# A hybrid attention and gated-DeltaNet layer: the 32-to-64 merge of the triangular inverses, four chunks at a time instead of one

## The chip, the cores and the metric

The kernel runs on one core of a Trainium2 chip. The metric is device time in microseconds (us) of one execution; the runs of the kernel before have a median of 1288.59 us (1287.44 to 1289.28, three runs). PE is the matrix engine, PEld its loading of the stationary operand, DVE, ACT and POOL are the vector, scalar and general engines, and SP is the engine whose queue issues most of the DMAs. "Lnnn" is a line of the kernel before.

## What is computed

One layer works on 1024 tokens of 1024 features. Two mixers share a normed input: a chunked band attention (8 heads of 64) and a gated DeltaNet (4 heads of 128). The change concerns the DeltaNet. Per chunk and head it needs

```
t_mat = a_strict + eye(CHUNK)                     # unit lower triangular
value       = triangular_solve(t_mat, v_beta)
k_cumdecay  = triangular_solve(t_mat, k_beta * exp(decay))
# then, chunk after chunk:
v_new = val - kc @ S
o     = qd @ S + att @ v_new
S     = S * cd + kt.T @ v_new
```

The reference uses chunks of 64 tokens, the kernel chunks of 128 (8 chunks, `c` = 0 to 7). In place of two triangular solves the kernel forms the inverse of the 128 x 128 matrix for each head, and multiplies by it. An output projection and a feed-forward part of width 4096 follow.

## The kernel before, in words

All matrix products of the big projections are done as three products of high and low parts. The program runs in four parts: the projections; attention beside the delta recurrence; the output projection; the feed-forward part. Everything below is in the first two.

**Two interleavings.** `interleave` takes turns among generators by the costs that they yield and a weight each. The first one runs the projections (`dq`, `dv`, gate, `ak`, `aq`, the first six tiles of `av`) with weight 1 and `delta_prep` with weight 0.35. The second one runs `attention` (weight 1), `delta_all` (2.0) and the last tiles of `av` (2.5). The order so written is a priority: a planner that simulates the program at build time then fixes the order of the instructions on every engine, and each engine's queue, SP's among them, works through that order strictly. An instruction later in the program can be put earlier where its operands and buffers are ready and the engine would stand idle.

**The inverse.** `delta_prep` computes the strict triangle A of each chunk, writes it to DRAM (`a_dr`, L521), reads the sixteen-per-chunk 32 x 32 diagonal blocks back (`ad`, L531), inverts all of them at once on DVE (L539, L543: 31 steps), and writes the inverses X and their transposes Y to DRAM (`x_dr`, `y_dr`, L548; 128-byte pieces). `delta_merge(c)` then makes the whole transposed inverse of one chunk:

- It loads A (L557, 256 KB), X and Y (L559, 64 KB each), clears the 128 x 512 page `m_yb` on POOL (L560) and copies the four diagonal blocks of Y into it (L563).
- From 32 to 64: the product p1 (L568, four matmuls, one per head, for the upper pair of blocks, then four for the lower pair), each half copied out by ACT (L570), and p2 (L577, the same numbers), each half written to `m_yb` by ACT with its sign turned (L578). A matmul is 32 x 32 or 64 x 32 of the array. It is executed as two records in the trace.
- From 64 to 128: transposes and products (L582, L584), a copy (L587), p4 (L592) and a last ACT write (L594).

Each chunk thus has four groups of eight records of the 32-wide form. A group and the ACT copy of its bank take turns, because both touch one PSUM bank. `m_p`, `m_tp`, `m_s`, `m_yb`, `m_ab` are the names of these tiles in the profile (p1, p2 and p4 are all `m_p`).

**The recurrence.** `delta_all` steps chunk by chunk through `delta_state` (S: `c_pk`, `c_pv`, `c_pq`, `c_pS`, all at L461 through the helper `four`), `delta_out` of the chunk before (O: `c_mt`, `c_po`), `delta_fin` (F: `c_tpo`), the merge of the next chunk (M) and the first step, that is the loads, of the merge after that (L), in the order of the string `ORDER = "OSMOSMFSOMOSMSL"`. All delta products share the two PSUM banks of `ps_d`. `c_pv` of chunk c reads the merged inverse of chunk c.

**Attention beside it.** `t_sb` and `t_sa` (L793) are scores, `t_tpb` and `t_tpa` (L844, L855) transposes, `t_o` (L865) values; `t_o` uses half of the array's columns (128*64 in the profile). Its queries are loaded as `t_q` (L774) on SP's queue.

Of the kernel before, what the change touches and what calls it, by code (L numbers as in the profile page):

```python
# [18 lines left out]
NT = SEQ // P  # L19
# [22 lines left out]
NV = 6  # L42
WV = 2.5
# [3 lines left out]
def hymba_kernel(  # L47
# [20 lines left out]
    nc = tc.nc  # L68
# [43 lines left out]
    ident = cpool.tile([P, P], F32, name="ident")  # L112
# [292 lines left out]
    def att_proj(u, col, kind, res=None):  # L405
        w = load_block(col, f"wa{kind}")
        for t in range(NT):
# [77 lines left out]
    def sumsq(sq, st, tp, n):  # L485
        nc.scalar.activation(sq, tp, AF.Square)
        ss = small(st, n + "_ss", 4)
        nc.vector.tensor_reduce(ss, b4(sq), AX.X, ALU.add)
        return ss
# [57 lines left out]
            for h in range(4):  # L547
                nc.sync.dma_start(out=dst[:, :, h, :], in_=src.rearrange("(q h) r e -> h q r e", h=4)[h])  # L548

    def delta_merge(c, res):  # L550

        n = f"m{c}"
        Ap, Yp, s1 = (page("pp", n + k) for k in ("_ab", "_yb", "_s1"))
        A, Y = b4(Ap), b4(Yp)
        X = s1[:, 384:512].rearrange("p (h e) -> p h e", h=4)
        Yc = s1[:, 256:384].rearrange("p (h e) -> p h e", h=4)
        nc.sync.dma_start(out=Ap, in_=a_dr[c])  # L557
        for dst, src in ((X, x_dr), (Yc, y_dr)):
            nc.sync.dma_start(out=dst, in_=src[4 * c:4 * c + 4].rearrange("b r h e -> (b r) h e"))  # L559
        nc.gpsimd.memset(Yp, 0.0)  # L560
        for b in range(4):
            bs = slice(32 * b, 32 * b + 32)
            nc.gpsimd.tensor_copy(Y[bs, :, bs], Yc[bs])  # L563
        yield 0
        p1 = bank(ps_d, n + "_p1")
        for c0 in (0, 64):
            for h in range(4):
                nc.tensor.matmul(p1[c0:c0 + 32, 32 * h:32 * h + 32], A[c0:c0 + 64, h, c0:c0 + 32],  # L568
                                 Y[c0:c0 + 64, h, c0 + 32:c0 + 64], start=True, stop=True)
            nc.scalar.copy(s1[c0:c0 + 32, 0:128], p1[c0:c0 + 32, 0:128])  # L570
        yield 500
        p2 = bank(ps_d, n + "_p2")
        for c0 in (0, 64):
            cs = slice(c0, c0 + 32)
            for h in range(4):
                hs = slice(32 * h, 32 * h + 32)
                nc.tensor.matmul(p2[cs, hs], X[cs, h, :], s1[cs, hs], start=True, stop=True)  # L577
            nc.scalar.mul(Y[cs, :, c0 + 32:c0 + 64], p2[cs, 0:128].rearrange("p (h e) -> p h e", h=4), -1.0)  # L578
        yield 500
        tp = bank(ps_d, n + "_tp")  # L580
        for h in range(4):
            nc.tensor.transpose(tp[0:64, h * 64:h * 64 + 64], Y[0:64, h, 0:64], ident[0:64, 0:64])  # L582
        for h in range(4):
            nc.tensor.matmul(tp[0:64, 256 + h * 64:320 + h * 64], A[64:128, h, 0:64], Y[64:128, h, 64:128],  # L584
                             start=True, stop=True)
        x1 = s1
        nc.scalar.copy(x1[0:64, :], tp[0:64, :])  # L587
        yield 700
        p4 = bank(ps_d, n + "_p4")
        for h in range(4):  # L590
            hs = slice(h * 64, h * 64 + 64)
            nc.tensor.matmul(p4[0:64, hs], x1[0:64, hs], x1[0:64, 256 + h * 64:320 + h * 64],  # L592
                             start=True, stop=True)
        nc.scalar.mul(Y[0:64, :, 64:128], p4[0:64, 0:256].rearrange("p (h e) -> p h e", h=4), -1.0)  # L594
        res[c] = Yp
        yield 400
# [90 lines left out]
    def delta_all(ab, kTs):  # L687

        Ys, D = {}, {}
        merge = delta_merge(0, Ys)  # L690
        yield from merge
        merge = delta_merge(1, Ys)
# [653 lines left out]
    for _ in delta_proj(u, DK, 4, "dk", None, kT, w_dk, first):  # L1346
        pass
    ab = ab_proj(u)
    after = []
# [58 lines left out]
```

## Time and profile before

| | |
|---|---|
| median of the runs | 1288.59 us (1287.44 to 1289.28) |
| the profiled execution: its own time | 1288.31 us |
| its span in the trace | 1286.6 us |
| mean granted TensorE clock | 0.998 |
| PE busy | 1260.6 us, 6702 records |
| DVE, ACT, POOL busy | 935.0, 553.9, 293.0 us |
| the merges' 32-wide groups: first and last start | 264.4 and 504.7 us |
| attention beside the recurrence | about 364 to 575 us |

The profiler records one execution. Times in its views count from the start of the span. In a timeline row the first number is the start, the second the length from the first record's start to the last one's end, then engine, line, operation, out<-in, the array's rows*columns in use, the operand's shape and the count. Records on PE overlap, so that the pace of PE is read from start to start, not from the durations.

### The profile page before, as it was taken

How to read it: one execution, taken by the hardware profiler on the slowest of the kernel's cores; microseconds unless marked ns; L12 is line 12 of the kernel's file. 1: busy time of each engine (PE TensorE's matmuls, PEld its weight loads, DVE VectorE, ACT ScalarE, POOL GpSimd, SP SyncE). 2: the span in 40 equal slices, each digit the busy share in tenths (PEclk: the TensorE clock that was granted, in tenths of full speed). 3: DMA queues.
4: the chain of work that ended last, by engine and by line, in shares of the span. 5: the costliest groups of instructions: out<-in, count | busy, mean ns of one | idle time of the engine just before them, and what ended most of it. 6: DMA issues, size and time to landing. Idle time of an engine off the chain costs nothing.

```text
span 1286.6 us, 18043 instructions
## 1 busy us (share of the span) xinstructions
PE 1260.6 (98%) x6702; PEld 1040.6 (81%) x6702; DVE 935.0 (73%) x1401; ACT 553.9 (43%) x919; POOL 293.0 (23%) x499
## 2 busy tenths in 40 slices
PE   9999999999999999989999999999999999999998
PEld 7778878788888887868877788888887888888886
DVE  7899987665046666863529876776668997897988
ACT  7233132133166664665335445444455443333331
POOL 4435461454024355523310000000000000000034
PEclk9999999999999999999999999999999999999999
DMA  6214353656492742125351433232358733422002
GB/s 223 61 44 140 100 164 112 145 147 160 144 270 79 218 109 75 42 65 163 122 166 31 151 116 129 98 110 97 105 196 318 238 93 104 131 86 95 17 33 98
DMA packets 129288, 160.65 MB, mean 125 GB/s; under 512 B 22832, under 2 KB 71984, under 8 KB 128688
## 3 DMA queue, kind: packets, MB, share of 16 engines
q1 hardware_dynamic: 111104, 137.20, 34.7%
q10 hardware_dynamic: 18096, 22.29, 5.0%
q8 instruction: 53, 0.87, 0.3%
q14 instruction: 35, 0.29, 0.1%
HBM read 111.75 MB, written 47.71 MB: 124 GB/s over the span
## 4 chain that ended last, share of the span: by engine, by line
PE 72%; DVE 8%; issue 2%; DMA 2%; POOL 1%; ACT 1%; POOLq 1%; SPq 0%; ACTq 0%; DVEq 0%
PE q L1087 22%; PE p L1183 20%; PE op L166 5%; PE av_ps L166 3%; PE aq_ps L166 3%; PE g_ps L166 3%; PE t_o L865 3%; PE ak_ps L166 2%; PE t_sb L793 1%; PE t_sa L793 1%; PE t_tpb L844 1%; PE t_tpa L855 1%; PE c_mt L461 1%; PE c_pS L461 1%; DVE ml L148 1%
## 5 line engine op out<-in xcount | busy, mean ns | idle before, releaser
L1255 POOL TENSOR_TENSOR y<-y,y 128x1024 f32<-128x1024 f32 x6 | 19.3, 3243 | 591.7 <-DVE y L1251 572.9
L1251 DVE TENSOR_TENSOR y<-y,p 128x1024 f32<-128x1024 f32 x46 | 55.2, 1218 | 5.4 <-PE p L1183 4.5
L808 DVE CUSTOM_DVE_ANT_0 t_pb<-t_sb,biasn 128x256 f32<-128x256 f32 (+1 forms) x64 | 25.4, 402 | 43.6 <-POOL biasn L720 25.4
L166 PE MATMUL op<-mh,wo_h 128*128 128x512 f32 x128 | 50.3, 393 | 0.8 <-DVE t_nm L808 0.3
L166 PE MATMUL op<-ml,wo_h 128*128 128x512 f32 x128 | 50.1, 391 | 0.0
L166 PE MATMUL op<-mh,wo_l 128*128 128x512 f32 x128 | 48.3, 391 | 0.0
L823 ACT ACTIVATE t_pb<-t_pb,t_nm 128x256 f32<-128x256 f32 (+1 forms) x64 | 31.6, 494 | 22.7 <-DVE t_nm L817 12.7
L966 DVE TENSOR_TENSOR h<-op,op_x 128x512 f32<-128x512 f32 x16 | 10.8, 688 | 30.7 <-PE op L166 30.7
L793 PE MATMUL t_sb<-ks,t_q 128*128 128x256 f32 (+1 forms) x144 | 30.4, 308 | 0.8 <-DMA t_q<-q_dr 0.5
L973 POOL TENSOR_TENSOR op_q<-op_q 128x512 f32<-128x512 f32 x14 | 20.1, 1439 | 48.0 <-ACT op_q L972 47.8
L166 PEld LDWEIGHTS op<-mh,wo_h 128*128 128x128 f32 x128 | 24.0, 188 | 7.4 <-issue 1.0
L817 DVE CUSTOM_DVE_ANT_0 t_pa<-t_sa,biaso,t_nm 128x384 f32<-128x384 f32 (+2 forms) x48 | 26.3, 547 | 4.4 <-PE t_sa L793 2.9
L865 PE MATMUL t_o<-t_ta,vt 128*64 128x128 f32 x240 | 27.3, 293 | 1.4 <-DVE t_ta L858 1.1
L166 PEld LDWEIGHTS op<-mh,wo_l 128*128 128x128 f32 x128 | 24.0, 188 | 5.2 <-issue 0.2
L166 PEld LDWEIGHTS op<-ml,wo_h 128*128 128x128 f32 x128 | 24.0, 188 | 4.9
L166 PE MATMUL g_ps<-uh,wg_h 128*128 128x512 f32 x64 | 25.2, 394 | 1.4 <-ACT wg_h L147 1.4
L826 ACT ACTIVATE t_pa<-t_pa,t_nm 128x384 f32<-128x384 f32 (+2 forms) x48 | 26.4, 550 | 0.1
L793 PE MATMUL t_sa<-ks,t_q 128*128 128x256 f32 (+2 forms) x128 | 25.5, 310 | 0.3 <-DVE t_nm L808 0.3
L166 PE MATMUL g_ps<-uh,wg_l 128*128 128x512 f32 x64 | 25.2, 394 | 0.4 <-POOL wg_l L148 0.4
L166 PE MATMUL dq_ps<-uh,wdq_h 128*128 128x512 f32 x64 | 25.5, 398 | 0.0
L166 PE MATMUL dv_ps<-uh,wdv_l 128*128 128x512 f32 x64 | 25.4, 397 | 0.0
L166 PE MATMUL aq_ps<-waq_h,uh 128*128 128x512 f32 x64 | 25.3, 401 | 0.0
(1102 smaller groups left out, 4353.8 us busy)
## 6 DMA issues: line engine op xcount, KB each, us to landing
wa<-in_w_ff_dram SPq DMA_DIRECT2D x32, 512.0 KB
a<-in_w_ff_dram SPq DMA_DIRECT2D x32, 512.0 KB
b<-f_dr SPq DMA_DIRECT2D x32, 512.0 KB
f_dr<-yy ACTq DMA_DIRECT2D x16, 512.0 KB
t_q<-q_dr SPq DMA_DIRECT2D x30, 256.0 KB
f_dr<-zz ACTq DMA_DIRECT2D x13, 512.0 KB
ks<-k_dr SPq DMA_DIRECT2D x16, 256.0 KB
wo_r<-in_w_out_dram SPq DMA_DIRECT2D x16, 256.0 KB
```

The source lines that it names most:

```text
L166: nc.tensor.matmul(ps, a, b, start=(i == 0), stop=(i == n - 1))
L461: nc.tensor.matmul(ps[:, hs], lhs(h, hs), rhs(h, hs), start=True, stop=True)
L793: nc.tensor.matmul(o, q[m][:, i * P:(i + 1) * P], k[:, c], start=(m == 0), stop=(m == 1))
L808: nc.vector.tensor_tensor_reduce(sb[:, c], bk[:, c], new[g][pp][:, c], -1.0, 3.0e38, ALU.add, ALU.min, nm[:, 4 + i:5 + i])
L817: nc.vector.tensor_tensor_reduce(sa[e][:, 0:wa], bk[:, 0:wa], old[g][i][:, 384 - wa:384], -1.0, nm[:, 4 + i:5 + i], ALU.add, ALU.min, nm[: ...
L823: nc.scalar.activation(sb[:, c], sb[:, c], AF.Exp, bias=m, scale=-1.0, accum_out=T["sums"][:, 4 + i:5 + i])
L826: nc.scalar.activation(sa[e][:, 0:wa], sa[e][:, 0:wa], AF.Exp, bias=m, scale=-1.0, accum_out=T["sums"][:, i:i + 1])
L865: nc.tensor.matmul(po[64 * e:64 * e + 64, pp * P:(pp + 1) * P], vt[k0 + j][:, 64 * h:64 * h + 64], (ta[e] if j < na else tb)[:, c:c + P], ...
L973: nc.gpsimd.tensor_tensor(acc, acc, sq, ALU.add)
L1087: nc.tensor.matmul(part(ps, q), l[:, s], r, start=(k + m == 0), stop=(k == 3 and m == 2))
L1183: nc.tensor.matmul(part(ps[q], 0) if by_rows else part(ps[q // 2], q % 2), l[:, s], part(r, k), start=(i + k + m == 0), stop=(i + k + m == 4))
L1251: nc.vector.tensor_tensor(y[i][m], y[i][m], ps[m], op)
```

## The change

`delta_merge` is split. A new generator `delta_low(b, W, tag)` does the step from 32 to 64 for the four chunks 4b to 4b+3 together. It clears two pages W on POOL, and loads with 32 DMAs on SP's queue: sixteen 32-row blocks of Y straight into their places in W, eight of X, and eight 32 x 32-per-head blocks of A (128-byte pieces, except X with 512). Then p1 is 16 matmuls for r0 = 0 and, after ACT's copy, 16 for r0 = 64, and p2 the same. The helper `held` puts the other 15 of such a group behind the first on PE's queue, at high priority. ACT copies 32 x 512 at once, and writes -p2 into W.

`delta_merge(c)` keeps the step from 64 to 128. It takes its operands from W, loads the lower left quarter of A (one DMA, 64 rows), and fills the final page `m_yb` with one POOL clear of 64 x 256 and two POOL copies of 64 x 256.

`delta_low(0)` is chained behind `delta_prep` in the first interleaving, with its pages from `pp`; `delta_low(1)` is chained ahead of the merge of chunk 4 in `delta_all` at c = 2, with its two working pages from `wh`.

```
+    def held(args, step):
+        first = step(*args[0])
+        with tc.issue_after(first.ins), tc.high_priority():
+            for a in args[1:]:
+                step(*a)
+
+    def delta_low(b, W, tag):
+        W += [page("pp", f"{n}_w{i}") for i in range(2)]
+        xa, s1 = page(tag, n + "_xa"), page(tag, n + "_s1")
...
+        for i in range(2):
+            nc.gpsimd.memset(W[-2 + i], 0.0)
+        for c in range(4):
+            q = 16 * b + 4 * c
+            for k in range(4):
+                nc.sync.dma_start(out=Y[c // 2][32 * k:32 * k + 32, c % 2, :, 32 * (k % 2):32 * (k % 2) + 32],
+                                  in_=y_dr[q + k])
+            for r0 in (0, 64):
+                nc.sync.dma_start(out=XA[r0:r0 + 32, c], in_=x_dr[q + r0 // 32])
+                nc.sync.dma_start(out=XA[r0 + 32:r0 + 64, c], in_=a4[c, r0 + 32:r0 + 64, :, r0:r0 + 32])
+        yield 0
+        places = [(c, h, slice(128 * c + 32 * h, 128 * c + 32 * h + 32)) for c in (3, 2, 1, 0) for h in range(4)]
+        p1 = bank(ps_d, n + "_p1")
+        for r0 in (0, 64):
+            rs, rs2 = slice(r0, r0 + 32), slice(r0 + 32, r0 + 64)
+            held(places, lambda c, h, hs: nc.tensor.matmul(
+                p1[rs, hs], XA[rs2, c, h, :], Y[c // 2][rs2, c % 2, h, 32:64], start=True, stop=True))
+            nc.scalar.copy(s1[rs], p1[rs])
+        yield 1000
+        p2 = bank(ps_d, n + "_p2")
+        for r0 in (0, 64):
+            rs = slice(r0, r0 + 32)
+            held(places, lambda c, h, hs: nc.tensor.matmul(
+                p2[rs, hs], XA[rs, c, h, :], s1[rs, hs], start=True, stop=True))
+            for i in range(2):
+                nc.scalar.mul(Y[i][rs, :, :, 32:64],
+                              p2[rs, 256 * i:256 * i + 256].rearrange("p (c h e) -> p c h e", c=2, h=4), -1.0)
+        yield 1000

-    def delta_merge(c, res):
+    def delta_merge(c, W, res):
...
+        nc.sync.dma_start(out=A[64:128], in_=a_dr[c].rearrange("r (h e) -> r h e", h=4)[64:128, :, 0:64])
+        nc.gpsimd.memset(Y[64:128, :, 0:64], 0.0)
+        nc.gpsimd.tensor_copy(Y[0:64, :, 0:64], Yd[0:64])
+        nc.gpsimd.tensor_copy(Y[64:128, :, 64:128], Yd[64:128])
...
-            merge = delta_merge(c + 2, Ys) if c + 2 < NT else iter(())
+            merge = delta_merge(c + 2, W, Ys) if c + 2 < NT else iter(())
+            if c == 2:
+                merge = chained(delta_low(1, W, "wh"), merge)
...
-        (delta_prep(kT, ab), 0.35))
-    interleave((attention(after[NV - 1]), 1.0), (delta_all(ab, kT), 2.0), (values, WV))
+        (chained(delta_prep(kT, ab), delta_low(0, W, "pp")), 0.35))
+    interleave((attention(after[NV - 1]), 1.0), (delta_all(ab, kT, W), 2.0), (values, WV))
```

More of the change, by code (lines that the diff above doesn't have):

```diff
@@ L548, in delta_prep @@
                 nc.sync.dma_start(out=dst[:, :, h, :], in_=src.rearrange("(q h) r e -> h q r e", h=4)[h])
-    def delta_merge(c, res):
-        n = f"m{c}"
[L553 to L563, printed above, removed]
-        yield 0
[L565 to L579, printed above, removed]
@@ new lines, in held @@
+    def held(args, step):
[4 more added lines that the diff above has]
+    def delta_low(b, W, tag):
+        n = f"l{b}"
+        W += [page("pp", f"{n}_w{i}") for i in range(2)]
+        xa, s1 = page(tag, n + "_xa"), page(tag, n + "_s1")
+        XA = xa.rearrange("p (c h e) -> p c h e", c=4, h=4)
+        Y = [w.rearrange("p (c h e) -> p c h e", c=2, h=4) for w in W[-2:]]
+        a4 = a_dr[4 * b:4 * b + 4].rearrange("c r (h e) -> c r h e", h=4)
+        for i in range(2):
[26 more added lines that the diff above has]
+        yield 1000
@@ new lines, in delta_merge @@
+    def delta_merge(c, W, res):
+        n = f"m{c}"
+        Yp, sa = page("pp", n + "_yb"), page("pp", n + "_sa")
+        Y = b4(Yp)
+        A = sa[:, 0:256].rearrange("p (h e) -> p h e", h=4)
+        Yd = W[c // 2].rearrange("p (c h e) -> p c h e", c=2, h=4)[:, c % 2]
+        nc.sync.dma_start(out=A[64:128], in_=a_dr[c].rearrange("r (h e) -> r h e", h=4)[64:128, :, 0:64])
+        nc.gpsimd.memset(Y[64:128, :, 0:64], 0.0)
+        nc.gpsimd.tensor_copy(Y[0:64, :, 0:64], Yd[0:64])
+        nc.gpsimd.tensor_copy(Y[64:128, :, 64:128], Yd[64:128])
+        yield 0
@@ L580, in delta_merge @@
         tp = bank(ps_d, n + "_tp")
         for h in range(4):
-            nc.tensor.transpose(tp[0:64, h * 64:h * 64 + 64], Y[0:64, h, 0:64], ident[0:64, 0:64])
+            nc.tensor.transpose(tp[0:64, h * 64:h * 64 + 64], Yd[0:64, h, :], ident[0:64, 0:64])
         for h in range(4):
-            nc.tensor.matmul(tp[0:64, 256 + h * 64:320 + h * 64], A[64:128, h, 0:64], Y[64:128, h, 64:128],
+            nc.tensor.matmul(tp[0:64, 256 + h * 64:320 + h * 64], A[64:128, h, :], Yd[64:128, h, :],
@@ L585, in delta_merge @@
                              start=True, stop=True)
-        x1 = s1
-        nc.scalar.copy(x1[0:64, :], tp[0:64, :])
+        nc.scalar.copy(sa[0:64, :], tp[0:64, :])
         yield 700
@@ L591, in delta_merge @@
             hs = slice(h * 64, h * 64 + 64)
-            nc.tensor.matmul(p4[0:64, hs], x1[0:64, hs], x1[0:64, 256 + h * 64:320 + h * 64],
+            nc.tensor.matmul(p4[0:64, hs], sa[0:64, hs], sa[0:64, 256 + h * 64:320 + h * 64],
                              start=True, stop=True)
@@ L685, in delta_fin, with delta_all @@
         yield 500
-    def delta_all(ab, kTs):
+    def delta_all(ab, kTs, W):
         Ys, D = {}, {}
-        merge = delta_merge(0, Ys)
-        yield from merge
-        merge = delta_merge(1, Ys)
+        yield from delta_merge(0, W, Ys)
+        merge = delta_merge(1, W, Ys)
         for c in range(NT + LATE):
@@ L1348, in hymba_kernel @@
     ab = ab_proj(u)
+    W = []
     after = []
```

## The prediction, made before the change was run

> **What bounds the kernel now.** I read the page's busy shares first, then the busy time by stretches of the stages that the change touches.
>
> ```profile
> PE 1260.6 (98%) x6702; PEld 1040.6 (81%) x6702; DVE 935.0 (73%) x1401; ACT 553.9 (43%) x919; POOL 293.0 (23%) x499
> ```
>
> ```profile
> 245.00:364.00 119.00, 119.00 (x590) 96.46 (x589) 46.92 (x110) 33.87 (x65) 43.40 (x67) 1.00 0.63 172
> 364.00:440.00 76.00, 76.00 (x741) 64.95 (x740) 46.09 (x160) 48.37 (x146) 27.93 (x74) 1.00 0.59 173
> 440.00:520.00 80.00, 76.31 (x743) 65.47 (x742) 52.44 (x159) 46.52 (x143) 39.11 (x100) 1.00 0.35 97
> 520.00:575.00 55.00, 50.01 (x422) 41.51 (x421) 41.77 (x111) 35.97 (x97) 22.03 (x61) 0.97 0.17 50
> ```
>
> The second fence gives stretch, length, then busy PE, PEld, DVE, ACT, POOL, granted clock, DMA share, GB/s. From 245 to 440 us PE has no idle time. From 440 to 575 it idles 3.7 and 5.0 us. No other engine comes near its limit there. So the time of these stages is PE's, and the question is what the merges' small matmuls cost on PE. Third, the merges' own instructions (busy times per record: minimum, median, maximum, in ns; first and last start).
>
> ```profile
> L568 PE MATMUL m_p<-m_yb,m_ab x128: 192/193/213, 264.4 to 501.4; 64*32 64x32 f32 x128
> L577 PE MATMUL m_p<-m_s x128: 191/191/212, 283.4 to 504.7; 32*32 32x32 f32 x128
> L570 ACT COPY m_s<-m_p x16: 249/256/258, 270.5 to 501.6; 32x128 f32<-32x128 f32 x16
> L578 ACT ACTIVATE m_yb<-m_p x16: 249/268/269, 318.0 to 504.9; 32x128 f32<-32x128 f32 x16
> ```
>
> 256 records in groups of 8 make 32 groups, four a chunk, all inside the stretch where PE is the bound.
>
> **The price of one group.** It is read from start to start in PE's timeline.
>
> ```profile
> 410.25 1.06 PE L461 MATMUL c_pk<-state,kT 128*128 128x128 f32 x8
> 411.24 0.43 PE L577 MATMUL m_p<-m_s 32*32 32x32 f32 x8
> 411.60 0.51 PE L793 MATMUL t_sb<-ks,t_q 128*128 128x256 f32 x2
> ...
> 509.04 1.06 PE L461 MATMUL c_po<-c_vn,c_att 128*128 128x128 f32 x8
> 509.94 0.38 PE L855 MATMUL t_tpa<-ident,t_pa 128*128 128x128 f32 x2
> ```
>
> A group takes 411.60 - 411.24 = 0.36 us until the next work starts. The eight `c_pk` ahead of it took 411.24 - 410.25 = 0.99, while eight equal matmuls before work of their own form took 509.94 - 509.04 = 0.90: 0.09 more, which I read as the array running empty before it changes its form. Behind a group, the next one pays as well:
>
> ```profile
> 370.24 0.66 PE L865 MATMUL t_o<-t_tb,vt 128*64 128x128 f32 x8
> 370.83 0.43 PE L577 MATMUL m_p<-m_s 32*32 32x32 f32 x8
> 371.19 1.16 PE L461 MATMUL c_pq<-state,c_jq 128*128 128x128 f32 x8
> ...
> 366.23 0.43 PE L568 MATMUL m_p<-m_yb,m_ab 64*32 64x32 f32 x8
> ...
> 481.44 0.44 PE L568 MATMUL m_p<-m_yb,m_ab 64*32 64x32 f32 x8
> ```
>
> `c_pq` is 1.16 long behind a group where `c_po` was 1.06: 0.10. One visit to the 32-wide form thus costs 0.09 + 0.36 + 0.10 = 0.55 us. Inside it the records follow at (0.43 - 0.19) / 7 = 0.034 us, so eight of them are only 0.27 us. The rest, 0.28 us, is paid per visit whatever its length.
>
> **Part by part.**
>
> *PE.* Before: 32 visits x 0.55 = 17.6 us. Eight of them (366.23 the first, 481.44 the last) stand beside a `t_o` of the 128*64 form, where the array would have to change its form anyway; there I take off 0.2, 1.6 us in all: 16.0. After: the same 128 matmuls, 256 records, in 8 visits of 32: p1 and p2, two halves each, twice. The halves stay apart, because ACT's copy and the next half share a bank. A visit is 0.09 + (31 x 0.034 + 0.19 - 0.07) + 0.10 = 1.36 us (0.07 is 0.43 - 0.36, what the next work overlaps): 10.9 us. Gain 5.1. If the visits beside `t_o` saved nothing, it would be 6.7; if the planner lets other work into the held groups and 16 visits result, about 16.0 - 13.1 = 2.9.
>
> *Waits of PE in the merges of the last chunks.*
>
> ```profile
> PE m_p L577 <- ACT m_yb L578: 0.8, 2, 0.4
> PE m_p L577 <- DVE c5q_ss L488: 0.5, 1, 0.5
> PE m_p L568 <- ACT m_s L570: 0.3, 1, 0.3
> ```
>
> These 1.6 us (us, times, longest) arise where little work is left to fill PE and p1, copy, p1, copy, p2 of one chunk follow each other. After the change chunks 4 to 7 are done at about chunk 3's turn, where PE never idles. I take half, 0.8 us, as gained: other waits will appear in their place. Bounds 0 and 1.6.
>
> *ACT.* Removed 16 x 0.256 + 16 x 0.268 = 8.4 us. Added: 4 copies of 32x512 and 8 writes of 32x256; the nearest rows are a 64x512 copy and a 64x256 write.
>
> ```profile
> L587 ACT COPY m_s<-m_tp x8: 567/578/580, 356.4 to 509.0; 64x512 f32<-64x512 f32 x8
> L594 ACT ACTIVATE m_yb<-m_p x8: 363/377/378, 362.4 to 514.6; 64x256 f32<-64x256 f32 x8
> L560 POOL MEMSET m_yb<- x8: 520/526/532, 247.1 to 478.6; 128x512 f32 x8
> L563 POOL COPY m_yb<-m_s x32: 279/286/293, 254.7 to 481.0; 32x128 f32<-32x128 f32 x32
> ```
>
> 4 x 0.578 + 8 x 0.377 = 5.3 us. ACT idles 28 of 76 us from 364 to 440: nothing either way on the path.
>
> *POOL.* Removed 8 x 0.526 + 32 x 0.286 = 13.4 us. Added: 4 clears of 0.526, 8 smaller ones of at most that, and 16 copies of 256 columns, between 0.286 and twice that: at most 2.1 + 4.2 + 9.2 = 15.5. POOL idles 48 of those 76 us; nothing. The copies no longer stand ahead of the merge's products, since these read W: that shortens the way to `c_pv`, which isn't what PE waits for in the list above. If POOL were late, `c_pv` would be.
>
> *SP's queue and the loads.* This is what the change adds.
>
> ```profile
> L531 SPq DMA_DIRECT2D ad<-a_dr x32: 262/352/399, 98.7 to 199.2; - x32
> L557 SPq DMA_DIRECT2D m_ab<-a_dr x8: 325/346/449, 200.1 to 470.3; - x8
> L559 SPq DMA_DIRECT2D m_s<-x_dr x8: 319/368/697, 248.4 to 473.2; - x8
> L559 SPq DMA_DIRECT2D m_s<-y_dr x8: 400/430/607, 251.8 to 473.5; - x8
> SPq L774 <- PE t_sb L793: 16.2, 3, 10.3
> SPq L774 <- PE c_tpq L465: 11.6, 1, 11.6
> SPq L774 <- PE t_on L887: 11.1, 1, 11.1
> SPq L774 <- PE c_Ltd L478: 8.1, 1, 8.1
> ```
>
> Removed: 8 x (0.346 + 0.368 + 0.430) = 9.2 us of issuing. Added: 64 loads of the kind of `ad` (16 KB, 128-byte pieces) at 0.352 = 22.5, and 8 quarters of A at 0.346 = 2.8. Net 16.1 us more, in two bunches of 32 x 0.352 = 11.3 us. The lower four rows (400 to 520 us) show the cover: SP stands 47 us before `t_q` loads because their page isn't free yet, in pieces of 8 to 11 us. A bunch that falls into one of them delays nothing; one that falls just after it puts the `t_q`, `c_jq`, `c_jv` and `c_kt` loads queued behind up to 11.3 us back, and PE's scores wait. In the first interleaving the bunch has to wait for the landing of `y_dr`, and the `k_dr` stores and the `waq` and `wav` weights are queued behind it. On PE itself the first product of a held group waits for the last load of its 32, and all of PE's queue stands behind it. Before, the last merge's loads were issued by 473.5, and the last record of its p1 started at 501.4: 28 us ahead, over twice a bunch. I take 0.5 us as the cost, with 0 and 11.3 as bounds.
>
> ```profile
> 240.00:250.00 10.00, 10.00 (x49) 8.21 (x48) 4.93 (x14) 2.33 (x4) 5.36 (x7) 1.00 0.91 159
> ```
>
> The transfers themselves: in this stretch the eight 128 KB stores of `x_dr` and `y_dr` go out in 128-byte pieces, 8192 of them, and the 16 DMA engines are 91% busy. If all of that were the small pieces, one would take 0.91 x 10 x 16 / 8192 = 0.018 us. Per bunch there are 3072 (24 loads of 128 pieces): at most 3.4 us of all 16 engines, beside a DMA share of 0.35 to 0.63. Half of the bytes go. No cost on the path.
>
> The Trainium skill speaks against this part: "DMA: Bandwidth & Descriptors", Rules for kernel authors, asks to coalesce small transfers into large ones, since under 64 KB mostly overhead is paid, and the Specifications there want pieces of 512 bytes. The stretch above agrees that small pieces keep the DMA engines busy at a low rate (159 GB/s at a share of 0.91); whether the overhead reaches PE no run here shows, and by that rule the sum would be that of the slower rival below.
>
> *Sum.* -5.1 - 0.8 + 0.5 = -5.4 us. Against the profiled execution's own 1288.31 us that is 1282.9; the median of the runs, 1288.59, lies 0.3 above it: 1283.2 us. What follows (output projection, feed-forward) starts from the end of this stage and moves with it.
>
> **The rivals.**
>
> *No gain: the tail takes it.* The visits that go from 440 to 520 us lie where PE idles already (3.7 us), and the eight long ones are all paid before 440, where every us counts. The groups of all `m_p` by stretch:
>
> ```profile
> 440.00:520.00 80.00, 8.78 (x144) 6.67 (x144) 5.16 (x18) 1.00 0.35 97
> ```
>
> Without the 32 records of four p4 that is 112 records, 14 visits behind 440: 14 x 0.55 = 7.7 us are freed there. If the recurrence and attention's own chain of scores, exponentials and transposes set the pace from there, that turns to idle PE time and only about 1 us is left: 1287.5. For it speaks that PE idles 5.0 of 55 us after 520; against, that from 440 to 520 it is 95% busy and its single waits are under 1 us. The same time results if the planner doesn't keep the held groups whole. 0.15.
>
> *Slower: SP's queue.* The mechanism is one bunch of loads issued ahead of a `t_q` (or weight) load whose page is free already. PE then has delta work for some us, and stands for the rest. It decides from the point where a bunch starts less than 11.3 us before the load behind it is needed. With 11.3 us lost once and the 5.1 gained: about 1288.6 - 5.1 + 11.3 = 1294.8; with half of it covered 1289 to 1290. For it speaks that one `t_q` load is already awaited by PE:
>
> ```profile
> PE t_sb L793 <- DMA t_q<-q_dr: 0.5, 1, 0.5
> ```
>
> Against it, the 47 us in which SP does nothing. 0.15.
>
> **How the numbers follow.** Forecast 1283.2 with 0.70, no gain 0.15, slower 0.15. A measurement of this kernel can tell about 0.2% (2.6 us) from no change. The forecast's own range is 1279 to 1286 (gain 2.9 with no wait removed, to 6.7 + 1.6 with no cost on SP, and another us where the order on the engines comes out differently). To hold 8 in 10 it is taken up to 1290, which covers no gain and half of the slower case, and down to 1278. Faster by over 0.2% 0.69, within 0.2% 0.17, slower 0.14.
>
> **What would show it.** Right: eight `p1`/`p2` groups of 32 records, start to next start near 1.18 us each, first of them near 265 us; PE's busy time lower by about 5 us from 364 to 575 and no new idle time; SP's waits for pages shorter by about 16 us. Wrong: PE waiting for the DMA into the new pages or for `t_q`, `waq`, `wav`; PE's idle time after 440 above 9 us by what it was freed of; or held groups broken up by 128-wide work.

## The result: slower by 0.8%, and the profile after

| | before | after |
|---|---|---|
| median of the runs beside each other | 1288.22 us (1287.44 to 1289.28, 4 runs) | 1298.45 us (1298.12 to 1299.92, 4 runs) |
| ratio, 95% interval | | 1.0081 (1.0066 to 1.0096) |
| span of the profiled execution | 1286.6 us | 1296.2 us |

The forecast was 1283.2 us. Lines of the changed kernel are numbered anew (`t_sb` L793 is L819 now, `t_o` L865 is L891, `mixd` L683 is L708, the `t_on` addition L888 is L914).

First the busy shares of the changed kernel, then its busy time in the stretches that the prediction used.

```profile
PE 1259.9 (97%) x6702; PEld 1038.4 (80%) x6702; DVE 933.5 (72%) x1401; ACT 551.3 (43%) x899; POOL 289.1 (22%) x487
```

```profile
245.00:364.00 119.00, 118.33 (x684) 97.26 (x683) 45.71 (x113) 35.42 (x66) 39.89 (x58) 1.00 0.60 162
364.00:440.00 76.00, 74.82 (x741) 65.57 (x740) 46.45 (x149) 44.42 (x129) 30.29 (x77) 1.00 0.63 174
440.00:520.00 80.00, 68.37 (x595) 58.06 (x594) 51.34 (x143) 36.26 (x95) 44.77 (x115) 1.00 0.29 81
520.00:575.00 55.00, 50.14 (x409) 38.44 (x410) 36.82 (x129) 42.14 (x134) 7.91 (x32) 1.00 0.20 57
```

Up to 440 us little is changed. From 440 to 520 PE is busy 68.37 us where it was 76.31, and executes 595 records in place of 743: new idle time of 8 us, which the prediction had named as a sign that it is wrong. Two tiles show whose work is late. First before, then after: the recurrence's `c_pS`, and attention's `t_o` (durations, then first and last start).

```profile
L461 PE MATMUL c_pS<-c_vn,c_kt x64: 275/275/377, 376.1 to 532.9; 128*128 128x128 f32 x64
L865 PE MATMUL t_o<-t_tb,vt x240: 272/273/411, 365.6 to 573.3; 128*64 128x128 f32 x120
```

```profile
L461 PE MATMUL c_pS<-c_vn,c_kt x64: 274/275/377, 372.3 to 501.3; 128*128 128x128 f32 x64
L891 PE MATMUL t_o<-t_tb,vt x240: 272/273/324, 370.2 to 582.3; 128*64 128x128 f32 x120
```

The recurrence ends 31.6 us earlier, attention 9.0 us later. The stage ends with attention. Everything behind it moves along: from the last `t_o` to the end of the span it is 713 to 714 us in both.

Now the hole. The changed kernel's timeline, PE's attention work and then the two kinds of results that DVE writes:

```profile
443.56 1.16 PE L819 MATMUL t_sa<-ks,t_q 128*128 128x128 f32 x8
478.43 0.60 PE L870 MATMUL t_tpb<-ident,t_pb 128*128 128x128 f32 x4
```

```profile
449.54 0.75 DVE L708 SCALAR_TENSOR_TENSOR mixd<-c_tpo,dng,c_jg 128x512 f32<-128x512 f32 x1 [0.86 <-PE c_tpo L465]
463.08 0.75 DVE L708 SCALAR_TENSOR_TENSOR mixd<-c_tpo,dng,c_jg 128x512 f32<-128x512 f32 x1 [0.75 <-PE c_tpo L465]
476.63 0.75 DVE L708 SCALAR_TENSOR_TENSOR mixd<-c_tpo,dng,c_jg 128x512 f32<-128x512 f32 x1 [0.75 <-PE c_tpo L465]
477.30 0.74 DVE L914 TENSOR_TENSOR t_on<-t_on,t_tot 128x256 f32<-128x256 f32 x2
```

Between 444 and 478 us no attention instruction runs on PE. The recurrence goes on alone, one chunk in 13.5 us (449.54, 463.08, 476.63): a chain of steps that each wait for the one before. The chain that ended last runs through it:

```profile
463.93 1.12 PE c_mt L461 x8
465.08 0.70 DVE c_att L688
465.78 0.14 issue
465.92 1.13 PE c_po L461 x8
467.05 0.91 PE c_pq L461 x8
467.98 0.69 DVE c_o L657
```

The two `t_on` additions start at 477.30, at the very end of the third `mixd`, and 1.1 us later attention is back. What ties them is a pool of pages. A `mixd` page (results of the recurrence, one for four chunks) and a `t_on` page (results of attention, one for four tiles) come from one pool, tag "m", six buffers. The planner hands out a tag's pages in the order in which the program first asks for them. The same additions and the first `mixd` of chunk 4 in DVE's own order, before and after (the number behind a name counts up with the program):

```
before:
L888 TENSOR_TENSOR t04_on_5069<-t04_on_5071,t04_tot_5066 128x256
...
L888 TENSOR_TENSOR t04_on_5069<-t05_on_5487,t05_tot_5483 128x256
...
L683 SCALAR_TENSOR_TENSOR mixd1_5113<-c4_tpo_5108,dng_290,c4_jg_4568 128x4x128
after:
L708 SCALAR_TENSOR_TENSOR mixd1_5102<-c4_tpo_5097,dng_290,c4_jg_4623 128x4x128
L914 TENSOR_TENSOR t04_on_5150<-t04_on_5152,t04_tot_5147 128x256
L914 TENSOR_TENSOR t04_on_5150<-t05_on_5491,t05_tot_5487 128x256
```

Before, the program asks for `t04_on` (5069) ahead of `mixd1` (5113). After, `mixd1` (5102) comes ahead of `t04_on` (5150). So attention's tiles 4 and 5 cannot hand over their results until chunk 4 of the recurrence has written its own. Both wait in the two PSUM banks that `t_tpb` of tile 6 needs.

Why did the program's order change? In the diff each `delta_merge` yields 700 and 400 where it yielded 500, 500, 700 and 400, and `delta_low(1)` yields 2000 once. In the second interleaving the eight merges and `delta_low(1)` declare 8 x 1100 + 2000 = 10800 where the merges declared 8 x 2100 = 16800. With a weight of 2.0 `interleave` therefore lets the recurrence run ahead of attention by 3000 of attention's units by the end.

### The profile page after: what moved, and what is told of

It reads as the page before. It is cut to its first block, busy times and chain, and to the rows that moved or that the text cites. A ratio compares the mean times of both kernels' runs of the same rounds, so it can differ in the third digit from the quotient of the medians.

```text
span 1296.2 us, 18079 instructions
## 1 busy us (share of the span) xinstructions
PE 1259.9 (97%) x6702; PEld 1038.4 (80%) x6702; DVE 933.5 (72%) x1401; ACT 551.3 (43%) x899; POOL 289.1 (22%) x487
## 4 chain that ended last, share of the span: by engine, by line
PE 57%; DVE 6%; ACT 2%; DMA 2%; issue 1%; POOL 1%; SPq 1%; POOLq 1%; ACTq 0%; DVEq 0%
PE q L1113 21%; PE p L1209 20%; PE op L166 5%; PE t_o L891 2%; PE t_sa L819 1%; PE t_tpa L881 1%; PE t_tpb L870 1%; PE t_sb L819 1%; DMA t_q<-q_dr 1%; PE c_po L461 1%; POOLq L1430 1%; DVE h L1054 1%; PE c_mt L461 0%; DVE y L1281 0%; DMA wo_r<-in_w_out_dram 0%
## 5 line engine op out<-in xcount | busy, mean ns | idle before, releaser
L1281 POOL TENSOR_TENSOR y<-y,y 128x1024 f32<-128x1024 f32 x6 | 19.4, 3246 | 592.1 <-DVE y L1277 573.3
L819 PE MATMUL t_sb<-ks,t_q 128*128 128x256 f32 (+1 forms) x144 | 28.8, 304 | 1.1 <-DMA t_q<-q_dr 0.8
L819 PE MATMUL t_sa<-ks,t_q 128*128 128x256 f32 (+2 forms) x128 | 26.6, 315 | 1.6 <-DVE t_nm L834 1.2
L891 PE MATMUL t_o<-t_ta,vt 128*64 128x128 f32 x240 | 26.5, 286 | 1.6 <-DVE t_ta L884 1.1
L873 ACT COPY t_tb<-t_tpb 128x512 f32<-128x512 f32 (+1 forms) x32 | 17.8, 558 | 20.9 <-PE t_tpb L870 20.9
```

The source lines that it names most:

```text
L819: nc.tensor.matmul(o, q[m][:, i * P:(i + 1) * P], k[:, c], start=(m == 0), stop=(m == 1))
L891: nc.tensor.matmul(po[64 * e:64 * e + 64, pp * P:(pp + 1) * P], vt[k0 + j][:, 64 * h:64 * h + 64], (ta[e] if j < na else tb)[:, c:c + P], ...
L1281: eng.tensor_tensor(y[i][m], y[i][m], y[z][m], ALU.add)
```

## The experiments

Theory A: the lowered declared costs, through the order of the pages, are the whole loss; the rest of the change is a gain. Rival B: the 64 loads on SP's queue make it (the prediction's slower rival). Rival C: the low step of chunks 0 to 3 now lies in the projections' stage, and the recurrence starts later for it. Each ratio is against runs of the kernel before on the same chip; microseconds are the ratio times 1288.2.

**e1: the change with the declared costs of before.**

```
-        yield 1000            (delta_low, twice)
+        yield 0 if b else 1000
-        yield 700   ...   yield 400        (delta_merge)
+        yield 1200  ...   yield 900
```

> The kernel after, with nothing changed but the costs that its generators declare to the interleaving: each merge declares 2100 in all, as before the change (1100 in the kernel after), and the low step of chunks 4 to 7 declares 0 (2000 in the kernel after). Theory A (the smaller declared costs let the recurrence run ahead in program order, so that the page for chunk 4's result, mixd1, is asked for before the page for attention tile 4, t04_on; attention then stands from about 444 to 477 us while the recurrence runs alone): the standstill goes, t04_on is written near 440 us, PE's idle time from 440 to 520 falls from 11.6 us to under 5, and the time is 1281 to 1287 us. Rival B (SP's queue: 64 small loads more): they are all still there, so 1295 to 1299. Rival C (the low step's work now lies in the projections' stage and the recurrence starts later): that is unchanged too, 1294 to 1299.

Measured: 1284.13 us (1282.31 to 1284.41), ratio 0.9965 (0.9953 to 0.9978): 4.5 us faster than before, 14.9 faster than the change as made. The busy time of the second interleaving, first in the changed kernel, then in e1, each up to its last `t_o`:

```profile
368.00:440.00 72.00, 70.82 (x718) 62.21 (x717) 46.02 (x147) 43.88 (x128) 29.55 (x73) 1.00 0.61 169
440.00:480.00 40.00, 32.70 (x276) 27.39 (x275) 22.72 (x53) 13.11 (x29) 26.54 (x65) 1.00 0.34 97
480.00:520.00 40.00, 35.67 (x322) 30.67 (x321) 28.62 (x90) 23.15 (x67) 18.23 (x50) 1.00 0.24 66
520.00:582.50 62.50, 55.91 (x465) 42.60 (x465) 41.72 (x135) 45.21 (x140) 11.65 (x38) 1.00 0.18 52
```

```profile
368.00:440.00 72.00, 70.68 (x729) 62.06 (x728) 46.24 (x152) 44.53 (x131) 30.18 (x76) 1.00 0.60 169
440.00:480.00 40.00, 37.89 (x340) 32.91 (x339) 22.76 (x74) 21.28 (x61) 17.91 (x42) 0.96 0.40 109
480.00:520.00 40.00, 39.15 (x349) 34.55 (x348) 32.31 (x99) 26.83 (x79) 21.68 (x59) 1.00 0.26 79
520.00:567.50 47.50, 42.49 (x369) 33.90 (x368) 36.92 (x99) 32.05 (x90) 16.76 (x49) 1.00 0.16 46
```

The same work (1781 and 1787 records) takes 214.5 us after and 199.5 in e1. PE's idle time in it is 19.4 against 9.3 us: 10 of the 15 us. The other 5 are busy time: about the same records are busy for 195.1 us against 190.2. I read that as records that overlap less where they come singly behind waits; it isn't shown by itself. Rival C falls here too: the first `c_pS` of the changed kernel starts at 372.3 us, earlier than the 376.1 of before.

**e2: nothing of the change, its lowered costs alone.** In the kernel before:

```
-        yield 500        (delta_merge, behind p1 and behind p2)
+        yield 0
```

> The kernel before, with nothing changed but two declared costs: the two steps of a merge that declared 500 each declare 0, so a merge declares 1100 as in the kernel after. Theory A: the order of the two pages turns round here as well, attention stands while chunks 3 to 6 run alone, and the time is 1294 to 1302 us although no instruction is added or removed. Rivals B and C: none of their causes is in this kernel, 1286 to 1290.

Measured: 1303.7 us (1301.59 to 1306.17), ratio 1.0122 (1.0104 to 1.0140), 15.7 us slower. The instructions are those of before, the program asks for `mixd1` (5053) ahead of `t04_on` (5179), and the hole stands at the same place, where PE was busy for 39.02 us before:

```profile
440.00:480.00 40.00, 31.12 (x308) 26.23 (x307) 21.58 (x48) 12.77 (x31) 24.38 (x59) 1.00 0.34 103
```

Two numbers of the program's text, which no engine ever executes, do more than all that the change does to the instructions.

**e3: the changed kernel with its own costs, and `t04_on`'s page asked for early.**

```
-                if t % TPH == 0:
-                    on = quarter(n + "_on")
-                    outs.update((t + i, part(on, i)) for i in range(TPH))
+            if not g and not t:
+                for k in range(2):
+                    on = quarter(f"{n}_on{k}")
+                    if k:
+                        nc.gpsimd.memset(on[:, 0:1], 0.0)
+                    outs.update((TPH * k + i, part(on, i)) for i in range(TPH))
```

> The kernel after with its own declared costs; only the page for the attention tiles 4 to 7 is taken ahead of all others, together with that for tiles 0 to 3 (one POOL clear of 128x1 added, which fixes when it is taken). Theory A in its narrow form (it is the page, not the recurrence's lead as such): 1281 to 1288 us, with t04_on written near 440 us. If the lead of the recurrence itself costs the time (too little left beside attention's end): 1291 to 1299. Rivals B and C: 1294 to 1299.

Measured: 1283.55 us (1280.4 to 1287.25), ratio 0.9964 (0.9944 to 0.9985). With the lowered costs left in, the order of two pages alone brings back the loss. That the stall is the page's is thereby shown, not argued.

**e9: the changed kernel with another weight.**

```
-    interleave((attention(after[NV - 1]), 1.0), (delta_all(ab, kT, W), 2.0), (values, WV))
+    interleave((attention(after[NV - 1]), 1.0), (delta_all(ab, kT, W), 1.8), (values, WV))
```

> The changed kernel with one number altered: delta_all's weight in the last interleave is 1.8 in place of 2.0, the declared costs stay as the change has them (1100 for a merge). In its program order t04_on comes ahead of mixd1 again. Theory (the lowered costs let the recurrence run ahead until t04_on's page waits behind mixd1's): the loss goes, with PE above 38 us busy in 440 to 480, and the time is 1281 to 1287. Rival: the loss comes from the loads or from the long groups, whatever the order: 1295 to 1300.

Measured: 1283.94 us (1281.08 to 1286.26), ratio 0.9972 (0.9961 to 0.9983). One number is the cheapest repair. The program asks for `t04_on` (5063) ahead of `mixd1` (5133) again, and PE is busy again:

```profile
440.00:520.00 80.00, 77.32 (x688) 67.38 (x687) 55.08 (x173) 47.88 (x138) 39.66 (x102) 0.98 0.33 94
```

**e5: the kernel before with 64 more loads of this kind on SP, which nothing reads.**

```
+    def extra_loads(b, tag):
+        t, v = (page(tag, f"x{b}_{i}").rearrange("p (c h e) -> p c h e", c=4, h=4) for i in "tv")
...
+                nc.sync.dma_start(out=t[32 * k:32 * k + 32, c], in_=a4[c, 32 * k:32 * k + 32, :, 32 * k:32 * k + 32])
...
+                nc.sync.dma_start(out=v[32 * k:32 * k + 32, c], in_=a4[c, 32 * k:32 * k + 32, :, 0:32])
```

> The kernel before with 2 x 32 loads of 32 rows in 128-byte pieces added on SP's queue, at the two places where the kernel after has its own (behind the inversion, and ahead of the merge of chunk 4); nothing reads them. The prediction's term for SP: 0.5 us with bounds 0 and 11.3, so 1287.5 to 1290. Theory A: no page order is turned, 1286 to 1290. Rival B: at least half of the loss, 1293 to 1299.

Measured: 1296.4 us (1295.34 to 1297.28), ratio 1.0064 (1.0050 to 1.0079): 8.2 us slower. That is what Rival B expected; Theory A's figure missed, and so did the prediction's term for SP (1287.5 to 1290). Its waits of PE:

```profile
PE t_sb L808 <- DMA t_q<-q_dr: 4.9, 2, 2.6
PE ak_tp L430 <- DVE ak_n L425: 3.1, 1, 3.1
```

The second bunch was issued from 397.7 to 419.3 us, with `t_q` loads behind it at 421.0. But most of the loss arises at the first bunch. All of these loads read A, which is ready early, so the first bunch is issued from 199.3 to 223.8 us, among the loads of the weights `wak` and `waq`. The changed kernel's loads of X and Y start at 247.6 us at the earliest. At the last `aq_ps` e5 is 5.4 us behind the kernel before (319.3 against 313.9), at the last `t_o` 7.0 (580.3 against 573.3).

Nor are the waits all of it. Behind the two longest, 3.1 and 2.6 us, PE's granted clock is lower for a few us:

```profile
200.00:245.00 45.00, 41.24 (x168) 32.62 (x167) 36.42 (x94) 9.32 (x16) 12.84 (x10) 0.92 0.45 118
400.00:440.00 40.00, 37.29 (x337) 31.93 (x336) 22.50 (x71) 21.54 (x59) 15.48 (x43) 0.96 0.51 138
```

Before, both stretches have 1.00. The wait for `ak_n` ends at 237.0 us; read in steps of 2 us the clock is 0.50 from 237 to 243, and the records of `ak_ps` follow at 0.43 us there and at 0.23 us before and behind. Over the two stretches that makes 45 x 0.08 + 40 x 0.04 = 5.2 us, an estimate, about as much as PE's added idle time in them (6.5 against 1.2 us). All four runs of e5 have a mean clock of 0.994 or 0.995, the runs of before beside them 0.996 to 0.999.

So e5 shows that such loads can cost 8 us, but not at the places of the change. In the changed kernel the same list has:

```profile
PE t_sb L819 <- DMA t_q<-q_dr: 0.8, 2, 0.6
...
PE l_p L580 <- DMA l_xa<-a_dr: 0.4, 1, 0.4
```

And e1, e3 and e9, which issue the change's 64 loads, are all faster than before: Rival B isn't the loss.

**e11: e1 with three loads per block in place of 32.** The pieces are of 512 bytes, of about the same bytes in all; the low step's blocks of A aren't loaded, and the inverses aren't the reference's.

```
-        for c in range(4):
-            q = 16 * b + 4 * c
...
+        for i in range(2):
+            nc.sync.dma_start(out=W[-2 + i][:, 0:256].rearrange("p (c x) -> p c x", c=2),
+                              in_=y_dr[16 * b + 8 * i:16 * b + 8 * i + 8].rearrange("(c k) r h e -> (k r) c (h e)", c=2))
+        nc.sync.dma_start(out=xa.rearrange("p (c x) -> p c x", c=4),
+                          in_=x_dr[16 * b:16 * b + 16].rearrange("(c k) r h e -> (k r) c (h e)", c=4))
```

> The kernel of e1 with three loads per block of four chunks in place of 32: whole stretches of y_dr and x_dr in pieces of 512 bytes, of about the same bytes, into the same pages. The values don't lie where the products need them and the quarters of A aren't loaded, so the inverses are not the reference's; all instructions of the other engines stay. It measures what the 64 loads cost by themselves. Theory (e1's 64 loads of 0.6 us on SP still cost about 4 us, which is what e8b stands above e8a): 1278 to 1281, and no wait of PE for t_q behind the bunch. Rival: the loads of e1 are covered, and e7's gain has another cause (its order): 1283 to 1285.

Measured: 1282.76 us (1279.77 to 1284.87), ratio 0.9967 (0.9953 to 0.9980), the ratio of e1. The two intervals leave about 0.0018 either way, 2.3 us. At the places where the change puts them, 58 of 64 loads gone bring nothing that can be measured within that. The theory of this expectation, 4 us, fell.

**e7: e1 with X loaded by two DMAs per block in place of eight.**

```
-                nc.sync.dma_start(out=XA[r0:r0 + 32, c], in_=x_dr[q + r0 // 32])
+            nc.sync.dma_start(out=XA[r0:r0 + 32], in_=xq[r0 // 32])
```

> The kernel of e1, but the inverses X of a block of four chunks are loaded by two DMAs (one for each half of the partitions) in place of eight: 26 loads of SP per block in place of 32. The loads took 0.6 us of SP each, so a bunch gets 3.6 us shorter. If the bunches still cost PE something in e1 (theory: up to the 0.7 us that the first product of the second block waits for its load, and waits for t_q behind the bunch), the time falls by 0.5 to 2 us: 1282 to 1283.6. Rival: in e1 the bunches lie in cover, and nothing changes: 1284 within 0.7.

Measured: 1280.11 us (1279.2 to 1282.05), ratio 0.9947 (0.9935 to 0.9959), the best version of the study and 0.53% faster than before. The intervals of e7 and e1 overlap, so that its 2.3 us over e1 are hardly clear of noise. After e11 the loads' time is an unlikely cause. The edit also puts the loads in another order on SP's queue. The profiled spans are alike, 1280.2 us and 1280.5 in e1, but e7's is of the longest of its five runs and e1's of the shortest. Why its time is below e1's, if it is, stays open.

**e10: e7 with the 52 loads on POOL's queue** (`nc.gpsimd.dma_start` in place of `nc.sync.dma_start`).

> The kernel of e7, with the 52 loads of the low step issued on POOL's queue in place of SP's. In e7 PE still waits 2.3 us for a t_q load that stands behind the second bunch on SP. If SP's queue is what is left of the loads' cost (theory), that wait goes and the time falls by 1 to 2.3 us against e7, to 1278 to 1279.5, as long as POOL, 23% busy, takes the issuing. Rival: the issuing costs POOL more than it cost SP, or POOL's own copies for the merges and c_y come later, and the time is that of e7 or above: 1280 to 1284.

Measured: 1291.19 us (1290.55 to 1293.05), ratio 1.0034 (1.0022 to 1.0047), slower, and above both expectations. A load takes POOL 0.548 us, and POOL's queue has other work behind it. One load stands 3.5 us at the head of that queue until the store of `ak_l` has landed:

```profile
POOL l_w L571 <- DMA k_dr<-ak_l: 3.5, 1, 3.5
```

DVE's longest wait for the key norm's step on POOL (`ak_y`) grows from 1.8 to 8.5 us. But little of that reaches PE as a wait: PE's own for `ak_n` is 1.4 us, where it was 1.2. What PE loses in this stage shows in its clock. First e7, then e10:

```profile
245.00:280.00 35.00, 35.00 (x273) 28.55 (x272) 18.71 (x39) 13.42 (x25) 17.90 (x20) 1.00 0.68 168
245.00:280.00 35.00, 33.17 (x249) 27.36 (x247) 13.32 (x30) 10.09 (x19) 24.58 (x36) 0.85 0.46 112
```

PE idles for 1.8 us there, and the granted clock of 0.85 costs about 35 x 0.15 = 5.2 us more, an estimate: 7 of the 11 us between e7 and e10. All five runs of e10 have a mean clock of 0.990 to 0.992, e7's 0.996 to 1.000. What brings the clock down just there stays open; no single wait of PE in the stretch is longer than 0.7 us. The expectation's reason fell as well. With none of these loads on SP, PE waits longer for `t_q` than the 2.3 us of e7, so that wait doesn't need the bunch on SP:

```profile
PE t_sb L821 <- DMA t_q<-q_dr: 3.9, 1, 3.9
```

**e6: e1 with its products chunk by chunk, in groups of eight records again.**

```
-        places = [(c, h, slice(128 * c + 32 * h, 128 * c + 32 * h + 32)) for c in (3, 2, 1, 0) for h in range(4)]
...
+        for c in range(4):
...
+                for h in range(4):
+                    nc.tensor.matmul(p1[rs, 32 * h:32 * h + 32], XA[rs2, c, h, :], Y[c // 2][rs2, c % 2, h, 32:64],
+                                     start=True, stop=True)
+                nc.scalar.copy(s1[rs, 128 * c:128 * c + 128], p1[rs, 0:128])
```

> The kernel of e1 (the changed kernel with the costs of before declared), but the low step's products are done chunk by chunk again: groups of four matmuls, eight records, as before, 32 of them in place of 8 long ones; copies of 32x128 by ACT; loads, pages, declared costs and the merge's later steps as in e1. If the long groups are what gained (theory: a visit to the 32-wide form costs about 0.55 us with eight records and 1.36 with 32), PE loses 32 x 0.55 - 8 x 1.36 = 6.7 us against e1, less up to 1.6 for groups beside a t_o: 5.1 to 6.7, so about 1289 to 1291. Rival: the gain of e1 over before comes from the merge's shorter chain (no copies on POOL ahead of its products) and from the order, and grouping is worth little: 1283 to 1286, within 1.5 us of e1.

Measured: 1284.6 us (1282.04 to 1288.1), ratio 0.9981 (0.9971 to 0.9992): 2.1 us above e1, with intervals that overlap. The time is in the rival's range, the difference a little over its 1.5 us. The planner runs neighbours together: 24 visits, ten in the first block and 14 in the second, not 32 (e1: 3 and 4 in the profile). Where they cost is seen by stage. First e1, then e6: from 245 us to the last `av_ps`, and from there to the last `t_o`.

```profile
245.00:367.70 122.70, 122.03 (x702) 100.24 (x701) 46.22 (x115) 36.06 (x68) 40.21 (x62) 1.00 0.60 165
367.70:567.50 199.80, 190.52 (x1779) 163.66 (x1777) 138.22 (x423) 124.98 (x361) 86.54 (x225) 0.99 0.39 110
```

```profile
245.00:370.40 125.40, 125.16 (x705) 100.07 (x704) 46.62 (x115) 38.56 (x80) 41.75 (x62) 1.00 0.60 163
370.40:569.80 199.40, 191.69 (x1779) 163.32 (x1778) 139.10 (x423) 126.53 (x368) 87.25 (x225) 1.00 0.39 109
```

In the first stage PE has hardly any idle time (0.67 and 0.24 us), and e6 takes 2.7 us longer. Of that, 0.6 isn't the visits': the `ak_tp` group next to 245 us starts at 245.43 in e1 and at 246.04 in e6, ahead of all of them. That leaves 2.1 us for seven more visits, 0.30 each, near the 0.28 that the prediction worked out. In the second, ten more visits add 1.2 us of busy time and nothing to the length, 199.4 against 199.8, as PE has 8 to 9 us of idle time there. (e1's granted clock is 0.99 there against 1.00, some 2 us at most, so that the ten visits may be worth up to that.)

**e8a and e8b: the 32-wide products left out**, in the kernel before and in e1. ACT copies from SBUF pages in their place; the lower 32-blocks of the inverses aren't computed. In e8a:

```
-                nc.tensor.matmul(p1[c0:c0 + 32, 32 * h:32 * h + 32], A[c0:c0 + 64, h, c0:c0 + 32], ...
-            nc.scalar.copy(s1[c0:c0 + 32, 0:128], p1[c0:c0 + 32, 0:128])
+            nc.scalar.copy(s1[c0:c0 + 32, 0:128], Ap[c0:c0 + 32, 0:128])
```

> The kernel before without its 32-wide products: the 256 records of a merge's p1 and p2 (lines 568 and 577) are left out, ACT copies from SBUF pages of the same shapes in their place, everything else stays; the inverses' lower 32-blocks are therefore not computed. It measures the price of the 32 visits by itself. Theory: 16.0 to 17.6 us of PE, all on the path, and 1.6 us of waits in the merge's chain: 1270 to 1273. Rival: a good part of the visits lies beside idle time or changes of form that are paid anyway, so that half or less is on the path: 1278 to 1282. Beside e8b: the falls' difference is what the grouping is worth.

> The kernel of e1 without its 32-wide products: the 256 records of the low step (lines 580 and 587) are left out, ACT copies from SBUF pages of the same shapes in their place; the inverses' lower 32-blocks are therefore not computed. Theory: 7 to 8 visits of 1.36 us, 9.5 to 10.9 us of PE, and the 0.7 us that the second block's first product waits for its load: 1273 to 1275. Rival: a bunch of loads that PE's chain no longer waits for moves the rest, or the visits are partly covered: 1276 to 1280. If the fall is smaller than e8a's by 5 us or more, the grouping is worth what the visits say; if by 2 or less, e6's reading holds.

Measured: e8a 1274.1 us (1273.37 to 1274.34), ratio 0.9898 (0.9885 to 0.9912); e8b 1277.95 us (1277.44 to 1279.02), ratio 0.9930 (0.9916 to 0.9943). In the kernel before the products cost 13.1 us of time, and e8a lies 1 to 2 us above the theory's range. Of PE's busy time they cost 15.3:

```profile
PE 1245.3 (98%) x6446; PEld 1028.0 (81%) x6446; DVE 932.8 (73%) x1401; ACT 553.7 (44%) x919; POOL 291.5 (23%) x499
```

In e1 they cost 0.35%, 4.5 us; e8b's time is in the range of its rival. But part of that fall is eaten in e8b by a wait that isn't among e1's:

```profile
PE aq_tp L430 <- DVE aq_n L425: 3.1, 1, 3.1
```

In e1 the first block's products stand where PE would otherwise wait for DVE's `aq_n`. Behind this wait the granted clock is lower too, 0.91 from 280 to 320 us, where e1 has 1.00; e8b's five runs have 0.994 to 0.996 on the mean, e1's 0.996 to 0.998. So the two falls can't simply be subtracted, and how much the grouping is worth can't be read from them.

## Why the prediction was wrong

**The step that failed** is one that the sum does not contain. "Part by part" costs instructions, loads and waits, but not the numbers that the generators yield, although the diff shows two `yield 500` of a merge removed. That the order might come out otherwise appears only in the range, as "another us where the order on the engines comes out differently". This was the term of +14.9 us (after against e1), and with it alone in the kernel before it is +15.7 (e2).

**PE's visits.** Right in mechanism and near in price; how much of it reached the time isn't settled. A long group in the changed kernel:

```profile
264.88 1.19 PE L580 MATMUL l_p<-l_w,l_xa 32*32 32x32 f32 x32
266.00 0.50 PE L166 MATMUL aq_ps<-waq_h,uh 128*128 128x512 f32 x1
...
271.03 1.10 PE L580 MATMUL l_p<-l_w,l_xa 32*32 32x32 f32 x29
...
272.06 1.08 PE L587 MATMUL l_p<-l_s,l_xa 32*32 32x32 f32 x29
273.06 0.66 PE L430 MATMUL ak_tp<-ident,ak_n 128*128 128x128 f32 x4
```

266.00 - 264.88 = 1.12 us from start to next start, where 1.18 was said; first at 264.9, where 265 was said. The second half of p1 and the first half of p2 ran as one visit (271.03 to 273.06), because p2's first half needs only the first copy. Seven visits in place of eight. The 16.0 us of the visits before were 15.3 of busy time (e8a). Of the predicted 5.1, e1 shows 4.5 as the whole change. How much of it is the visits isn't settled: e6 gives them 2.1 us in the first stage and between nothing and 2 us in the second. This is the mechanism of the first rival (freed time that turns to idle time), for a part of the visits. The whole difference of e6 to e1, 2.1 us, is hardly clear of noise, so the nearness of 4.5 to the forecast's 5.4 is no proof of its terms. e6, with 24 visits, is still 2.4 us faster than before. That part of the gain lies in what e6 shares with e1: the first block's products moved ahead into the first stage, merges without p1 and p2 in their chain, and visits merged by the planner. Which of these it is, no run shows.

**Waits of PE in the merges.** Of the 1.6 us of before, 0.8 was to go. In e1, where no hole disturbs the list, 1.0 is left:

```profile
PE m_p L617 <- ACT m_sa L612: 0.7, 1, 0.7
...
PE m_p L617 <- DVE c_jv L644: 0.3, 1, 0.3
```

**Held groups.** Built without `held`, e1 has the same instruction order on all five engines: the helper does nothing here. This was seen in the order, not run.

**SP's queue.** The unit price was wrong; the term isn't contradicted. Rows of the changed kernel:

```profile
L570 SPq DMA_DIRECT2D l_w<-y_dr x32: 538/597/1197, 250.1 to 390.7; - x32
L574 SPq DMA_DIRECT2D l_xa<-a_dr x16: 544/573/642, 199.5 to 416.1; - x16
L573 SPq DMA_DIRECT2D l_xa<-x_dr x16: 419/585/716, 247.6 to 415.5; - x16
```

A load takes 0.6 us of SP, where 0.352 had been taken from `ad`, a load with other partitions: 38 us in all, not 22.5. Still PE waited for loads in the changed kernel only the 0.4 and 0.8 us quoted under e5, of which 0.5 was there before. In e1, where no hole stretches the stage, it waits longer:

```profile
PE t_sb L819 <- DMA t_q<-q_dr: 2.7, 2, 2.1
...
PE l_p L580 <- DMA l_xa<-a_dr: 0.7, 1, 0.7
```

The 2.1 us end at 463.6 us, 48 us behind the last load of the bunch. In e11, with 6 loads in place of 64, a wait of 1.6 us stands there still, and in e10, with none of them on SP, one of 3.9. So the bunch doesn't explain it; its cause stays open. The predicted +0.5 fits, and e11 can tell it from nothing no better than to some 2 us. The slower rival's 1294.8 came near the measured time by another mechanism; its own is real (e5) where a bunch stands just ahead of a load that is needed. By the rule of the Trainium skill that the prediction cited ("DMA: Bandwidth & Descriptors", Rules for kernel authors: coalesce small transfers) e11 should have gained: three loads of 512-byte pieces ran no faster than 32 of mostly 128. Small transfers off the path cost nothing here that these runs could measure.

**ACT and POOL.** The new instructions took what was estimated, and PE's list of waits names none of them. In the changed kernel ACT's copies of 32x512 took 577 ns and its writes of 32x256 368 ns, where 578 and 377 had been put; POOL's copies took 392 ns, put between 286 and 572.

**The tail.** The prediction held that it could at worst take back the gain. In fact the stage's end is set by attention and not by the recurrence: the recurrence came 31.6 us earlier and that bought nothing.

## What to carry to other kernels

Costs that generators declare to an interleaver are part of a change: when a diff moves or deletes a `yield`, work out how far the other streams shift, before costing a single instruction. Where two streams draw pages from one tag, compare the order in which they first ask for them, before and after: a swap can stall a whole stream behind an unrelated one. And price a saved visit, or a load, at the stage where it lies: a visit was worth 0.30 us where PE had hardly any idle time, and between nothing and 0.2 us where it had some. When a run is slower than its waits explain, read the granted clock by stretches before looking for another cause.

## What the runs showed of the hardware that was not expected

- Issuing a load of 32 partitions in 128-byte pieces takes SP about 0.6 us (0.597, 0.573), in 512-byte pieces as well (0.585), against 0.352 for the loads `ad` of equal size; on POOL's queue the same loads take 0.548.
- Inside a long group the 32 x 32 records follow at about 32 ns (1.00 us from the first to the last of 32), and the next 128-wide record starts 0.12 us behind the last.
- A long wait of PE can cost more than itself, since the granted clock can be at 0.50 for a few us behind it: 237 to 243 us in e5, behind a wait of 3.1. In the changed kernel's hole PE idles 7.3 of 40 us, in waits of at most 0.9, and the clock stays at 1.00 from 440 to 480. Between these the runs show no sharp border: behind the 2.1 us of e1 it falls (0.96 from 440 to 480), behind 2.2 us at 466 in e5 it doesn't (1.00 from 440 to 480).
